# Neighbourhood attention: the second part of the keys in a tile of its own for each head, with zeros in the other 64 rows

## The chip, the cores and the metric

The kernel runs on one core of a Trainium2 chip. The metric is the device time of one execution in microseconds. One execution was also recorded by the hardware profiler; its span is the time from the first to the last instruction.

## The reference

Two layers of a diffusion block over 512 latent tokens (a grid of 8 rows and 64 columns) and 256 context tokens, 1024 features. Each layer mixes the tokens with four groups of heads (gated delta rule, short convolution, long convolution, neighbourhood attention), each 256 features wide, and joins them in one output projection; an MLP follows. The change lies in the neighbourhood attention, with 4 heads of 64 features. Cut to what matters:

```python
qb = qx.reshape(bsz, N_HEADS, rows, ncb, NA_QCOLS, HEAD_DIM) * scale
s_win = jnp.einsum("bhrnqd,bhrwnkd->bhrnqwk", qb, kb)       # 16 query columns against 32 key columns, all 8 rows
s_win = jnp.where(valid[:, :, None, :], s_win + bias, NEG)
s_ctx = jnp.einsum("bhrnqd,bhcd->bhrnqc", qb, kc)           # and against the 256 context tokens
p_all = jax.nn.softmax(jnp.concatenate([s_win..., s_ctx], axis=-1), axis=-1)
o = einsum(p_win, vb) + einsum(p_ctx, vc)
```

In the first layer the context tokens attend to each other as well.

## The kernel before

Large products run on operands split into two parts of a reduced float format, a high part and the small rest, so that high times high, high times rest and rest times high together give nearly the full precision (`mm3`, lines 138 to 140).

`na_project` writes the parts of queries and keys, and the values, to scratch in DRAM. `na_heads` reads them back. It loops over the two pairs of heads (`pr`); for each pair, per head (`sub`), the tile `naq` holds on 64 rows the first part of the queries and on the other 64 rows their second part, and `nak` holds the first part of the keys twice, on both halves. One product over 128 rows (line 1198) thus sums both parts of the queries against the first part of the keys. The second part of the keys, for both heads of the pair, lies in one tile `nakl`; a second product (line 1199) adds the queries' first part times it, on the 64 rows of that head.

A unit is one block of 128 queries of one head. For `n` below 4 the queries are 16 columns of the grid, with two score products of 256 columns each (window, context); in layer 0 the blocks `n` = 4 and 5 are context tokens, with one. That makes 24 units in layer 0, with 40 pairs of lines 1198 and 1199, and 16 units with 32 pairs in layer 1. After the scores of a unit come, in turn: the bias `nab` added on VectorE (line 1207, its load is line 1206), the maximum (1209), the exponential on ScalarE (1212), the reciprocal (1213), the scaling (1217 on ScalarE, or 1215 on VectorE), four transposes on TensorE (1220), the copy of the result to `PT` on ScalarE (1222), and the products with the values (1229), which for the two heads fill 64 columns of the array each. The values come through `vw`, a copy by GpSimd (1174) of a column window of `nav`, transposed on TensorE (1180).

All loads go through SP's queue, in order. Each engine's order is fixed when the program is built, by a planner that weighs dependencies and free buffers; it places the short convolution's products (tiles mc and mx of lines 138 to 140) and others between the units. A tile's tag names a ring of buffers: a new tile of that tag waits until the users of the oldest one are done. `deep` is 0 in layer 0 and 1 in layer 1. GpSimd's zeroing of another tile, line 877, and the modulation rows of line 254 appear in the prediction as well; line 126 and 127 make the two parts of a block of weights.

Of the kernel before, what the change touches and what calls it, by code (L numbers as in the profile page):

```python
# [45 lines left out]
class Net:  # L46
# [24 lines left out]
    def setup(self):  # L71
# [7 lines left out]
        # minus one on one block of 32 or 64 partitions  # L79
# [50 lines left out]
    def split(self, x, y, r):  # L130
        """x as two parts, into the columns r of the pair y."""
        self.nc.scalar.copy(y[0][:, r], x)
        self.nc.vector.tensor_sub(y[1][:, r], x, y[0][:, r].bitcast(F32))

    def mm3(self, o, st, mv, first, last):
        """o (+)= st.T @ mv with both operands as sums of two parts."""
        mmul = self.nc.tensor.matmul
        mmul(o, st[0], mv[0], start=first, stop=False)  # L138
        mmul(o, st[0], mv[1], start=False, stop=False)  # L139
        mmul(o, st[1], mv[0], start=False, stop=last)  # L140

    def pair(self):
        """Two banks of PSUM."""
        return self.pb.tile([128, 2, 512], F32, tag="pb", name="pb", bufs=3)

    def big(self, wsrc, acts, segs):
        """Products of one block of output features; returns a PSUM tile per token range."""
# [19 lines left out]
    def mod_first(self, p, i, act, cb=None):  # L167
        """One block of the shift (i < 2) or scale of the first norm. Few rows: four parts of the sum share the
        array's columns. The weights of some blocks lie where the normed activations will go."""
# [29 lines left out]
    def first_scale(self, XS, p):  # L199
        """Each block of 128 features of the input: features onto partitions, in place, with unit norms."""  # L200
# [39 lines left out]
    def cond_rows(self, p):  # L240
        """The activated conditioning vectors as rows on every partition."""
        self.cbc = p.tile([128, 2, D], F32, tag="cbc", name="cbc")
        self.junk = p.tile([128, 512], BF16, tag="junk", name="junk")
        self.ring(p, "ad", 2)
        self.nc.sync.dma_start(self.cbc, self.cdr[0].partition_broadcast(128))

    def mod_steps(self):
        """One step per block of rows."""
# [19 lines left out]
    def ring(self, p, tag, bufs):  # L268
        """Where the blocks of modulation weights are loaded from now on."""
# [7 lines left out]
    def fac_pre(self, l, i, cnd, k0=0, k1=KB):  # L277
        """gain * (1 + m) of the norm before a sub-layer; i = 0 mixing, 1 mlp."""
# [4 lines left out]
    def fac_post(self, l, i, cnd, p):  # L283
        """gain * m of the norm after a sub-layer, as a row on every partition."""
# [21 lines left out]
    def post_norm(self, Y, row, X, out, p):  # L306
        """out = X + norm(Y) * gain * m for one block of tokens; returns what ends it, which returns a free buffer."""
# [14 lines left out]
    def finish(self, t, mm, ws, Y, row, X, p, before):  # L322
        """The last products and norm of one block of tokens, by halves of the features; before() ends the block
        before. Returns what ends this one."""
# [23 lines left out]
    def pre_scale(self, X, t, p):  # L348
        """The identity times the reciprocal norms."""
# [5 lines left out]
    def pre_norm(self, l, i, xs, p, out, off, cnd, dgs=None):  # L355
        """Features onto partitions; h = norm(x) * gain * (1 + m) + m' as two parts."""
# [59 lines left out]
    def filters(self, ld, p):  # L416
        """The filter networks up to their last hidden layer, two side by side on the partitions: both layers' of the
        long filter, and both halves of the short one's times."""
# [19 lines left out]
    def spectrum_loads(self, l, L, p):  # L438
        """What a filter's spectrum is made from."""
# [10 lines left out]
    def spectrum(self, hs, ld, l, L, p):  # L450
        """Spectrum of a two-sided filter at the odd frequencies and the norm of each channel."""
# [35 lines left out]
    def spectra(self, dft, uc, us, L, p, sp):  # L487
        """The cosine and sine sums over the even and odd times, E +- O, at the odd frequencies:
        [128 k, (C+, C-, S+, S-), k block, channel]. The frequencies of the second block mirror those of the first:
        there the sums over the times 1 and 3 modulo 4 trade cosines for sines, the others only signs."""  # L490
# [5 lines left out]
        if nk == 2:  # L496
            # (source, cosines or sines, parity, where the sum and the difference go)
# [39 lines left out]
    def hyena_project(self, l, w_in, hx, segs, p):  # L537
        """The convolved projections: x1 * v (two blocks) and x0 (two blocks)."""
# [21 lines left out]
    def hyena(self, l, u, x0, segs, ydst, p):  # L560
        nc, a = self.nc, self.a
        for off, L in segs:
# [43 lines left out]
            # the sums of both blocks that belong to each residue of the time: [(residue, cosine or sine)]  # L606
# [25 lines left out]
    def gdn_project(self, l, nm, j0, w_in, hx, segs, psum):  # L632
        """One of q, k and v: projected, convolved, activated and turned to tokens on partitions."""
# [18 lines left out]
    def gdn_rates(self, l, w_ab, hx, segs, p):  # L652
        """The logs of decay and beta, tokens on partitions. Few columns: four groups of them share the array,
        each with its part of the sum."""
# [27 lines left out]
        def rates(after):  # L682
# [6 lines left out]
            # log(1 + e) = log(w) + (e - (w - 1)) / w with w = fl(1 + e)  # L689
# [13 lines left out]
    def gdn_normalise(self, tok, p, rates):  # L703
        """Unit norm and rotary of keys and queries in place."""
# [44 lines left out]
    def gdn_solve(self, l, tok, la, lbeta, p, values):  # L749
# [3 lines left out]
        # feature-major q and k: [2 heads x 64, pair, tokens]  # L753
# [13 lines left out]
        # cumulative log decay, forward and backward, and the total of each block  # L767
# [47 lines left out]
    def gdn_systems(self, kT, qT, nq, p, ip):  # L815
        """Per direction, block and head: the system's strictly triangular part, transposed, and the query
        weights."""
# [35 lines left out]
    def gdn_inverse(self, UX, p, ip):  # L853
        """UX holds N (strictly triangular parts and a diagonal that is ignored); becomes (I + N)^-1."""
        nc = self.nc
        # the diagonal 32-blocks; slots without a system still pass through the 32 x 32 transposes
# [5 lines left out]
        for dr in range(2):  # L862
# [6 lines left out]
            # the blocks with rows before columns for the first direction, after for the second: both lower  # L869
            nc.vector.transpose(S[:, dr] if dr == 0 else S[:, dr].rearrange("p j i -> p i j"),  # L870
                                G[:, dr].rearrange("p u i -> p i u"))
        # the blocks between the halves go apart, zeros in their place and on the diagonal
# [9 lines left out]
        # substitution inside the 32-blocks, both directions at once  # L882
# [7 lines left out]
        # back: G[32 b + j, u, i] = T[i, j] and its transpose GT  # L890
# [11 lines left out]
    def gdn_levels(self, UX, G, GT, Xt, BB, ip):  # L902
        """From the inverses of the 32-blocks to those of 64 and of 128. Every sum runs over all partitions, with
        zeros in all but one block, which keeps the array at its full clock; the directions and blocks work on
        different columns of it at the same time."""
# [4 lines left out]
        def lower(zp, w, signs):  # L910
            """The products of one stage, negated; a part per block of partitions."""
# [11 lines left out]
        # 32 -> 64: block (a, b) of each pair  # L923
# [38 lines left out]
        # 64 -> 128  # L962
# [25 lines left out]
    def gdn_chain(self, dr, X, qk, ring, tok, seen, nq, p):  # L988
        """The blocks of one direction in turn; yields between stages, so that two directions can alternate.
        The sum of both directions takes the place of the queries."""  # L990
# [13 lines left out]
        def decayed(st):  # L1004
            """Keys and queries times their decay from the start of the block, features on partitions."""
# [109 lines left out]
    def na_project(self, w_in, hx, segs, full, dst):  # L1115
        """Queries and keys as two parts, and the values; one step per block of output features."""
# [26 lines left out]
    def na_heads(self, l, src, y, p, pn, with_ctx):  # L1143
# [7 lines left out]
        for pr in range(2):  # L1151
# [3 lines left out]
            # per head: both parts of the queries, and the keys' first part against each; the keys' second part  # L1155
            # lies with the queries' first
            kl = p.tile([128, T], F32R, name="nakl", tag="nakl")
            nc.sync.dma_start(kl.bitcast(F32), src["k", pr, 1])
            qs, ks = [], []
            for sub in range(2):  # L1160
                q = p.tile([128, T], F32R, name="naq", tag=f"naq{sub}")
                k = p.tile([128, T], F32R, name="nak", tag=f"nak{sub}")
                rows = slice(64 * sub, 64 * sub + 64)
                for half in range(2):
# [4 lines left out]
                ks.append(k)  # L1169
            vk = p.tile([128, 10, 128], F32, name="vk", tag="vk")  # L1170
            for n in range(5):
                if n < 4:
                    vw = p.tile([128, 256], F32, name="vw", tag="vw", bufs=2)
# [9 lines left out]
            for n in range(nq):  # L1183
# [3 lines left out]
                for sub in range(2):  # L1187
                    h = 2 * pr + sub
                    rows = slice(64 * sub, 64 * sub + 64)
# [7 lines left out]
                    def score(o, keys):  # L1197
                        nc.tensor.matmul(o, q, keys(ks[sub]), start=True, stop=False)  # L1198
                        nc.tensor.matmul(o, q[rows], keys(kl)[rows], start=False, stop=True)  # L1199
# [4 lines left out]
                    if n < 4:  # L1204
                        bias = p.tile([128, 256], F32, name="nab", tag="nab", bufs=3)
# [18 lines left out]
                # the heads share the array's columns  # L1224
# [59 lines left out]
    def mix(self, l, hx):  # L1284
# [17 lines left out]
        with self.pool("tok") as self.tp:  # L1302
# [12 lines left out]
            with self.pool("gdn") as gp:  # L1315
# [9 lines left out]
                with self.pool("psg", 4, space=PSUM) as self.pg, self.pool("pso", space=PSUM) as self.po:  # L1325
                    na = self.na_project(w_in[14:20], hx, segs, full, nad)

                    def others(n):
                        """Work that fills the gaps of the inverse, and the values."""
# [28 lines left out]
    def mlp(self, l, ysp, ysp_s):  # L1358
# [7 lines left out]
        def runs(ts):  # L1366
            """Neighbouring tiles with the same modulation."""
# [266 lines left out]
def _blocks(w, nb):  # L1634
    """[K, N] -> [N / 128, 128, K / 128, 128]: one contiguous tile per block of outputs."""
# [4 lines left out]
def _layout(x, c, ctx, c_ctx, ada_w, ada_b, norm_pre_mix, norm_post_mix, norm_pre_mlp, norm_post_mlp,  # L1640
# [34 lines left out]
    # relative position bias, gathered for the queries (row, column) of a column block and its key window  # L1675
# [34 lines left out]
```

## Time and profile before

| | us |
|---|---|
| three runs, median | 1896.51 |
| lowest and highest of them | 1891.33 and 1897.97 |
| profiled execution, span | 1898.1 |
| TensorE busy in it | 1804.4 |
| VectorE busy in it | 1269.1 |
| ScalarE busy in it | 775.0 |

No other time of the profiled execution is given beside its span. Busy times of TensorE are modelled at their ends, since matmuls are pipelined: the distance between the starts of two matmuls tells more than the duration of one. A wait is put down to the work that ended it. PE is TensorE's matmuls, PEld its weight loads, DVE VectorE, ACT ScalarE, POOL GpSimd, SP the engine that issues the loads.

### The profile page before, as it was taken

To read this page: it belongs to the slowest core of one execution; us is meant where nothing else is said; L and a number is where in the kernel's file an instruction comes from. 1 tells how busy PE (TensorE), PEld (TensorE's weight loads), DVE (VectorE), ACT (ScalarE), POOL (GpSimd) and SP (SyncE) were. 2 spreads that over 40 slices of the span, in tenths; PEclk is the share of its full clock that TensorE was granted. 3 is DMA by queue.
4 is the path that set the end of the run, shared out by engine and by line. 5 is a ranking of instruction groups with operands and counts; after the bars stand their busy time and mean duration, and the time that the engine had idled before them with its cause. 6 is when DMAs were issued, how large, how long until landed. Compare 5 with 4: busy or idle time off the path is not lost. (4 is left out here: it accounts for less than half of the span.)

```text
span 1898.1 us, 29470 instructions
## 1 busy us (share of the span) xinstructions
PE 1804.4 (95%) x11170; PEld 1450.4 (76%) x11170; DVE 1269.1 (67%) x2366; ACT 775.0 (41%) x1547; POOL 256.7 (14%) x265
## 2 busy tenths in 40 slices
PE   5899888999999999999999999998899999999998
PEld 2577777777779888888888876777676788777876
DVE  3888989665766777755555586779856665454545
ACT  4433553366556222222222263363346563332323
POOL 0202441500022000000000041152230110000002
PEclk9999999999999999999999999989999999999999
DMA  8452312344555434444434233112233664232322
GB/s 276 145 177 83 121 42 98 120 134 129 166 181 180 146 116 127 131 125 128 133 124 132 78 130 131 62 64 84 77 98 112 194 198 127 83 117 72 106 89 83
DMA packets 107073, 233.54 MB, mean 123 GB/s; under 512 B 14929, under 2 KB 19859, under 8 KB 105652
## 3 DMA queue, kind: packets, MB, share of 16 engines
q1 hardware_dynamic: 106932, 231.67, 38.7%
q8 instruction: 88, 1.44, 0.3%
q14 instruction: 53, 0.43, 0.1%
HBM read 208.41 MB, written 23.21 MB: 122 GB/s over the span
## 5 line engine op out<-in xcount | busy, mean ns | idle before, releaser
L126 ACT CAST whi<-raw 128x512 fp32r<-128x512 f32 x444 | 273.6, 620 | 671.6 <-PE pb L140 261.8
L127 DVE TENSOR_TENSOR wlo<-raw,whi 128x512 fp32r<-128x512 f32 x444 | 316.9, 720 | 215.9 <-ACT whi L126 209.7
L140 PE MATMUL pb<-acth,wlo 128*128 128x512 f32 (+2 forms) x808 | 282.6, 350 | 0.0
L139 PE MATMUL pb<-actl,whi 128*128 128x512 f32 (+2 forms) x808 | 282.2, 349 | 0.0
L138 PE MATMUL pb<-acth,whi 128*128 128x512 f32 (+2 forms) x808 | 281.4, 348 | 0.0
L138 PE MATMUL pb<-whi,hid 128*128 128x512 f32 x628 | 249.6, 397 | 0.1
L139 PE MATMUL pb<-wlo,hid 128*128 128x512 f32 x628 | 248.7, 396 | 0.5 <-DVE wlo L127 0.4
L140 PE MATMUL pb<-whi,hid 128*128 128x512 f32 x628 | 248.6, 396 | 0.0
L1497 DVE TENSOR_TENSOR acc<-acc,pb 128x1024 f32<-128x1024 f32 x96 | 117.2, 1221 | 150.5 <-PE pb L140 149.5
L258 DVE SCALAR_TENSOR_TENSOR junk<-adrow,cbc 128x512 bf16<-128x512 f32 x256 | 181.1, 707 | 5.1 <-DMA adrow<-in_adaD_dram 1.8
L139 PE MATMUL mx<-actl,whi 128*128 128x512 f32 x416 | 174.3, 419 | 1.4 <-POOL actl L374 1.1
L138 PE MATMUL mx<-acth,whi 128*128 128x512 f32 x416 | 170.3, 410 | 2.1 <-ACT acth L235 1.2
L140 PE MATMUL mx<-acth,wlo 128*128 128x512 f32 x416 | 171.7, 413 | 0.5 <-DVE wlo L127 0.4
L138 PEld LDWEIGHTS pb<-acth,whi 128*128 128x128 f32 x808 | 152.5, 189 | 20.3
L139 PEld LDWEIGHTS pb<-actl,whi 128*128 128x128 f32 x808 | 152.1, 188 | 20.1
L140 PEld LDWEIGHTS pb<-acth,wlo 128*128 128x128 f32 x808 | 152.5, 189 | 19.7
L374 POOL TENSOR_TENSOR actl<-et,acth 128x256 fp32r<-128x256 f32 (+2 forms) x64 | 56.1, 892 | 745.1 <-DVE et L373 740.4
L138 PEld LDWEIGHTS pb<-whi,hid 128*128 128x128 f32 x628 | 117.7, 187 | 32.4 <-ACT hid L1398 5.1
L140 PEld LDWEIGHTS pb<-whi,hid 128*128 128x128 f32 x628 | 117.8, 188 | 29.5 <-DVE hid L1399 1.8
L139 PEld LDWEIGHTS pb<-wlo,hid 128*128 128x128 f32 x628 | 117.8, 188 | 28.7 <-DVE wlo L127 1.6
L138 PEld LDWEIGHTS mx<-acth,whi 128*128 128x128 f32 x416 | 79.9, 192 | 20.1 <-ACT acth L235 1.6
L139 PEld LDWEIGHTS mx<-actl,whi 128*128 128x128 f32 x416 | 80.5, 194 | 19.1 <-POOL actl L374 1.8
(396 smaller groups left out, 3033.7 us busy)
## 6 DMA issues: line engine op xcount, KB each, us to landing
raw<-in_w_dram SPq DMA_DIRECT2D x276, 256.0 KB, 2.9
adrow<-in_adaD_dram SPq DMA_DIRECT2D x80, 512.0 KB, 3.7
raw<-in_win_dram SPq DMA_DIRECT2D x104, 256.0 KB, 2.8
raw<-in_wout_dram SPq DMA_DIRECT2D x64, 256.0 KB, 3.0
X<-xdr SPq DMA_DIRECT2D x14, 512.0 KB, 4.6
X<-in_xin_dram SPq DMA_DIRECT2D x12, 512.0 KB, 4.4
xdr<-X SPq DMA_DIRECT2D x10, 512.0 KB, 2.9
adp<-in_adaP_dram SPq DMA_DIRECT2D x16, 256.0 KB, 5.4
```

What stands on the lines that cost most here:

```text
L126: self.nc.scalar.copy(hi, raw)
L127: self.nc.vector.tensor_sub(lo, raw, hi.bitcast(F32))
L138: mmul(o, st[0], mv[0], start=first, stop=False)
L139: mmul(o, st[0], mv[1], start=False, stop=False)
L140: mmul(o, st[1], mv[0], start=False, stop=last)
L258: nc.vector.scalar_tensor_tensor(self.junk, raw[:, hs], 1.0, self.cbc[:, cnd, hs], op0=OP.mult, op1=OP.mult, accum_out=self.part[:, l, cnd ...
L374: nc.gpsimd.tensor_sub(lo[:, r], t, hi[:, r].bitcast(F32))
L1497: op = nc.vector.tensor_add(o, o, ps)
```

## The change

The second part of the keys gets a tile for each head (`nakl0`, `nakl1`). Its 64 rows of that head are loaded from DRAM; GpSimd writes zeros to the other 64 rows. Line 1199's product then runs over all 128 rows of `naq`: the rows with the queries' second part meet zeros. The loads of the second part become two of 64 rows instead of one of 128. `vw` no longer has a ring of two buffers of its own, but shares that of the biases `nab`, which has two buffers in layer 0 and three in layer 1, where the biases alone had three in both. The rest of the diff takes comments out.

```diff
@@ -1152,25 +1152,27 @@
             e = T if with_ctx else TX
             vt = p.tile([128, T], F32, name="nav", tag="nav")
             nc.sync.dma_start(vt, src["v", pr])
-            # per head: both parts of the queries, and the keys' first part against each; the keys' second part
-            # lies with the queries' first
-            kl = p.tile([128, T], F32R, name="nakl", tag="nakl")
-            nc.sync.dma_start(kl.bitcast(F32), src["k", pr, 1])
-            qs, ks = [], []
+
+
+            qs, ks, kls = [], [], []
             for sub in range(2):
                 q = p.tile([128, T], F32R, name="naq", tag=f"naq{sub}")
                 k = p.tile([128, T], F32R, name="nak", tag=f"nak{sub}")
+                kl = p.tile([128, T], F32R, name="nakl", tag=f"nakl{sub}")
                 rows = slice(64 * sub, 64 * sub + 64)
+                nc.gpsimd.memset(kl[64 - 64 * sub:128 - 64 * sub].bitcast(F32), 0.0)
+                nc.sync.dma_start(kl[rows].bitcast(F32), src["k", pr, 1][rows])
                 for half in range(2):
                     hr = slice(64 * half, 64 * half + 64)
                     nc.sync.dma_start(q[hr, :e].bitcast(F32), src["q", pr, int(half != sub)][rows, :e])
                     nc.sync.dma_start(k[hr].bitcast(F32), src["k", pr, 0][rows])
                 qs.append(q)
                 ks.append(k)
+                kls.append(kl)
             vk = p.tile([128, 10, 128], F32, name="vk", tag="vk")
             for n in range(5):
                 if n < 4:
-                    vw = p.tile([128, 256], F32, name="vw", tag="vw", bufs=2)
+                    vw = p.tile([128, 256], F32, name="vw", tag="nab", bufs=2 + deep)
                     nc.gpsimd.tensor_copy(vw.rearrange("p (r c) -> p r c", c=32),
                                           vt[:, :TX].rearrange("p (r c) -> p r c", c=64)[:, :, starts[n]:starts[n] + 32])
                 else:
@@ -1186,7 +1188,6 @@
                 PTs = []
                 for sub in range(2):
                     h = 2 * pr + sub
-                    rows = slice(64 * sub, 64 * sub + 64)
                     unit += 1
                     if not with_ctx and unit % 3 == 0:
                         sc = self.pm.tile([128, nk], F32, tag="mc", name="sc", bufs=self.mbufs[1])
@@ -1196,13 +1197,13 @@
 
                     def score(o, keys):
                         nc.tensor.matmul(o, q, keys(ks[sub]), start=True, stop=False)
-                        nc.tensor.matmul(o, q[rows], keys(kl)[rows], start=False, stop=True)
+                        nc.tensor.matmul(o, q, keys(kls[sub]), start=False, stop=True)
                     if n < 4:
                         score(sc[:, 0:256].rearrange("p (r c) -> p r c", c=32),
                               lambda k: k[:, :TX].rearrange("p (r c) -> p r c", c=64)[:, :, starts[n]:starts[n] + 32])
                     score(sc[:, nk - 256:nk], lambda k: k[:, TX:T])
                     if n < 4:
-                        bias = p.tile([128, 256], F32, name="nab", tag="nab", bufs=3)
+                        bias = p.tile([128, 256], F32, name="nab", tag="nab", bufs=2 + deep)
                         nc.sync.dma_start(bias, a["nab"][l, h, variant[n]])
                         nc.vector.tensor_add(sc[:, 0:256], sc[:, 0:256], bias)
                     mx = p.tile([128, 1], F32, name="mx", tag="mx", bufs=4)
```

## Rows read from the trace of the kernel before

**Rows 1.** Page, part 1: busy time, share of the span, instructions.

```profile
PE 1804.4 (95%) x11170; PEld 1450.4 (76%) x11170; DVE 1269.1 (67%) x2366; ACT 775.0 (41%) x1547; POOL 256.7 (14%) x265
```

**Rows 2.** Windows: width, busy PE, PEld, DVE, ACT, POOL (instructions), PEclk, DMA share, GB/s.

```profile
400.00:430.00 30.00, 30.00 (x183) 21.46 (x181) 20.29 (x57) 20.86 (x50) 0.00 (x0) 1.00 0.37 114
430.00:470.00 40.00, 39.99 (x246) 28.64 (x244) 20.00 (x57) 25.41 (x64) 0.81 (x2) 1.00 0.44 122
...
1420.00:1460.00 40.00, 40.00 (x234) 27.41 (x233) 23.50 (x60) 28.56 (x66) 1.06 (x2) 1.00 0.45 128
```

**Rows 3.** Timeline of PE: start, duration, line, operation.

```profile
391.74 0.28 PE L1198 MATMUL sc<-nak,naq 128*128 128x256 f32 x1
391.95 0.38 PE L1199 MATMUL sc<-nakl,naq 64*128 64x256 f32 x1
392.26 0.38 PE L1198 MATMUL sc<-nak,naq 128*128 128x256 f32 x1
...
393.11 0.28 PE L139 MATMUL mc<-actl,whi 128*128 128x256 f32 x1
393.23 0.28 PE L140 MATMUL mc<-acth,wlo 128*128 128x256 f32 x1
...
394.41 0.40 PE L138 MATMUL mx<-acth,whi 128*128 128x512 f32 x1
```

**Rows 4.** Chain that ended last, 1405 to 1475 us, by line.

```profile
by line: PE op L1229 15.3%; PE sc L1199 14.3%; PE mx L139 11.7%; PE pt L1220 11.1%; PE sc L1198 11.1%; PE mx L140 10.5%; PE mx L138 10.5%; DMA raw<-in_wout_dram 5.1%; PE pt L1180 3.8%; issue 1.9%; ACT ysp L132 1.6%; ACT frow L295 1.5%; DVE 
```

**Rows 5.** Instructions of line 1199 and line 1198: ns min/median/max.

```profile
L1199 PEld LDWEIGHTS sc<-nakl,naq x72: 182/183/183, 391.9 to 1459.5; 64*128 64x128 f32 x72
L1198 PEld LDWEIGHTS sc<-nak,naq x72: 186/186/192, 391.5 to 1459.2; 128*128 128x128 f32 x72
```

**Rows 6.** Timeline of PE around line 1229.

```profile
406.67 0.28 PE L140 MATMUL mc<-acth,wlo 128*128 128x256 f32 x1
406.88 0.43 PE L1229 MATMUL op<-PT,vk 128*64 128x128 f32 x2
...
443.62 0.39 PE L1199 MATMUL sc<-nakl,naq 64*128 64x256 f32 x1
443.94 0.43 PE L1229 MATMUL op<-PT,vk 128*64 128x128 f32 x2
```

**Rows 7.** Windows of line 1199 alone: busy PE and PEld (instructions).

```profile
400.00:430.00 30.00, 6.11 (x16) 2.93 (x16) 1.00 0.37 114
...
1420.00:1460.00 40.00, 9.93 (x26) 4.75 (x26) 1.00 0.45 128
```

**Rows 8.** Waits, 391 to 470 us: total, times, longest.

```profile
DVE sc L1207 <- PE sc L1199: 14.5, 13, 3.1
...
PEld op L1229 <- ACT PT L1222: 1.8, 7, 0.4
```

**Rows 9.** Page's DMA part: KB each, us from issue to landing.

```profile
nab<-in_nab_dram SPq DMA_DIRECT2D x32, 128.0 KB, 2.4
nak<-nak SPq DMA_DIRECT2D x16, 192.0 KB, 5.0
...
nakl<-nak SPq DMA_DIRECT2D x4, 384.0 KB, 3.9
```

**Rows 10.** Waits of SP's queue, 384 to 470 us.

```profile
SPq L1206 <- DVE sc L1207: 32.4, 11, 8.0
```

**Rows 11.** Timeline of layer 1's second pair.

```profile
1441.89 0.43 DVE L1207 TENSOR_TENSOR sc<-sc,nab 128x256 f32<-128x256 f32 x1 [0.44 <-PE sc L1199]
...
1442.80 0.44 PE L1180 MATMUL pt<-cst,vw 128*128 128x128 f32 x2
```

**Rows 12.** GpSimd's memset of line 877; timeline of the first vw.

```profile
L877 POOL MEMSET BB<- x4: 1377/1586/1792, 251.5 to 1283.8; 64x1536 f32 x4
...
381.97 0.74 POOL L1174 COPY vw<-nav 128x256 f32<-128x256 f32 x2 [12.11 <-PE ops L1068]
...
385.32 0.60 PE L1180 MATMUL pt<-cst,vw 128*128 128x128 f32 x4
```

## The prediction

> **What bounds the kernel now.** I read the page first: TensorE counts as busy for 95% of the span, more than any other engine [rows 1]. Then I cut out the two stretches in which the scores are made, 391 to 470 us (layer 0) and 1405 to 1470 us (layer 1), because a share over the whole span says nothing about them. In three windows there TensorE has no idle time, at a granted clock of 1.00 (the level of 2.4 GHz), while VectorE and ScalarE are busy 50 to 71% [rows 2]. A busy TensorE is no TensorE at its peak, since the ends of its matmuls are modelled; so I read next the starts in its timeline [rows 3]. There the reader is to see two paces. The short convolution's 128-row products of 256 columns (lines 138 to 140, tile mc) start 0.118 us after one another: eleven intervals from 393.11 to 394.41 are 1.30 us. The scores have the same 256 columns, but around each line 1199, whose operands have 64 rows, the pace is 0.21 us before it and 0.31 us after it. The chain that ended last goes through the same instructions: in 1405 to 1475 us lines 1199 and 1198 hold 14.3% and 11.1% of it, and no other engine has a share as large [rows 4]. So a TensorE interval saved here is on the path that sets the end.
>
> **The second product on 128 rows.** Line 1199 stays one instruction for each product, 72 in all [rows 5], with the same 256 columns. The weight load takes 186 ns on 128 rows against 183 ns on 64, so the taller operand costs nothing that the rows show. What can go is the pause on both sides of the 64-row shape. From 391.74 to 393.11 there are five products in 1.37 us [rows 3]; at the pace of 0.118 us they would take 0.59. Two line 1199 thus cost 0.78 us extra, 0.39 each. 72 times 0.39 is 28.1 us. Behind 7 of the 72 in the timeline comes line 1229, which fills 64 columns of the array, 0.32 us later in the case shown; a part of that pause stays, since behind a 128-row product line 1229 also comes only after 0.21 us [rows 6]. 0.21 instead of 0.12 at one end, and no pause of the next 128-row product to save, are 0.19 us less in each, 1.3 us for 7. Gross gain: 26.8 us, some 15 in layer 0 (40 products) and 12 in layer 1 (32). Its bounds are 0, if the 0.31 us belongs to something that stays, and 28. I take 26.8, because the pause follows every one of the 72 whatever comes next and whichever bank it writes, and none of the 128-row products around them.
>
> A rule speaks against the edit: the Trainium skill, TensorEngine Tiling (Array Packing), section Performance Considerations (When to Use Tiling), would have a contraction of 64 rows use half of the array, so that two such products run beside each other. By it the zeros give away up to half of the work of 72 products, 36 times 0.118 = 4.2 us, and the kernel would end near 1901. The trace does not bear it out for this order: the heads' 64-row products never stand side by side, a 128-row product is always between them, and the pace is the slower one [rows 3]. The Trainium skill's same page, section Key Properties, has a change of the tiling mode drain the engine, which agrees with these rows.
>
> **What lies behind the gain: the softmax.** TensorE's order is fixed when the program is built, so less work between scores and transposes means less cover for the softmax. In 1420 to 1460 us stand 26 line 1199 [rows 7]: 26 times 0.39 is 10.1 us, which leaves 29.9 of 40, and ScalarE is busy 28.6 us in it [rows 2], 96%. In 400 to 430 us 16 of them leave 23.8 us beside 20.9 of ScalarE, 88%; in 430 to 470 us some 20 leave 32.2 beside 25.4, 79%. Nowhere does ScalarE exceed what is left, but at 96% work in a fixed order waits for each other. TensorE already waits for it in small pieces, 1.8 us for the copies of PT in layer 0 [rows 8]. Lower bound of the loss: nothing, for the planner can put convolution products between. Upper bound: the 10.1 us of the tight stretch and half of layer 0's gain, 17 us. I take 4 us, 3 of them in layer 1.
>
> **The shared ring of nab and vw.** Before, the biases had three buffers and vw two of its own; now they share two in layer 0 and three in layer 1. Within a pair of heads a bias load can be issued only when line 1207 of the unit two before has ended; it takes 2.4 us to land [rows 9]. A unit makes two line 1199, so 1420 to 1460 us hold 13 units, 3.1 us each, and 2.3 us each when shortened [rows 7]: two of them, 4.6 us, are nearly twice what the load needs, and in layer 0 the units are no faster. All 13 waits of line 1207 are for the scores, none for a bias [rows 8]. SP's queue already stands 32.4 us at the head of these loads [rows 10], and what is queued behind it are weights for line 126, the next modulation rows and the second pair's keys. At the change of the pair the ring costs more: the second pair's four vw copies must wait for the first pair's last biases, and its first biases for the transposes of vw. In layer 1 the second group of these transposes stands at 1442.8 us, and line 1207 needs its first bias at 1441.9 [rows 11]; a load issued behind it lands over 3 us late, unless the planner moves the transposes up. In layer 0 the context units (n = 4 and 5), which use no bias, stand between. Bounds: nothing, and 4 us in each layer. I take 3 us together.
>
> **Zeros and loads.** Eight memsets of 64x768 on GpSimd: half of line 877's 64x1536, 1.59 us, so 0.79 us each [rows 12]. GpSimd is idle there; two of them stand before the vw copies at 381.97 us and make them 1.6 us later; the copies end at 382.7 and TensorE first reads them at 385.3, so I take nothing. Without that cover it is 1.6 us a pair, 6 us in all. The whole load of nakl (384 KB) becomes two halves. The nearest rows are nak's halves, which land 5.0 us after their issue against 3.9 for the whole nakl [rows 9]: if the first scores of each of the four pairs wait for that, it costs 4 times 1.1, 4.4 us. But the first unit no longer needs the second head's half, and convolution products stand before the first scores, so I take nothing, with 4.4 us as the bound. The Trainium skill, DMA: Bandwidth & Descriptors, section Rules for kernel authors, advises against two transfers to the two halves of the partitions, which it says serialize; by it those 4.4 us would be paid and the sum would be 15.6 us. The rows on landing lean that way, but show nothing that waits for it.
>
> **The sum.** 26.8 less 4 less 3 is 20 us. The profiled execution spans 1898.1 us, so 1878; the page gives no other time for it. The median of the three runs is 1896.5, 1.6 less, so I predict 1876.5. The runs themselves lie within 0.35%; 0.5%, 9.5 us, is about what can be told from no change.
>
> **The rivals.**
> 1. The softmax takes the place of the pauses. For: ScalarE at 96% of the shortened stretch. Against: TensorE waits little for it now. With the upper loss of 17 us, and 3 for the ring, 7 us are left: 1890.
> 2. The whole gain is kept, or a new order gives more: 1866 to 1870. For: TensorE has no real waits there now.
> 3. The change does not remove the pause, because strided keys or accumulation into the same bank makes it: 1896 to 1898. Against: the contiguous keys have it too, and products into other banks after it.
> 4. Slower: the ring of two in layer 0. If each bias load waits behind another load in SP's queue until its scores are done, a unit pays 2.4 us of landing, 16 units 38 us, and 12 us are lost in the end: about 1908. It decides from 1.7 us of lateness a unit (27 over 16). Against: the loads are issued two units ahead.
> 5. Half-row products are the cheap ones: the pauses have another cause and stay, and the zeros add 36 times 0.118, 4.2 us: 1901. Against: the pace around a lone 64-row product is the slower one [rows 3]. (The Trainium skill, TensorEngine Tiling (Array Packing), When to Use Tiling, is the rule behind it.)
>
> **How the numbers follow.** The forecast (1872 to 1884) has 0.55; rival 1 0.18, two thirds of it below 1887; rival 2 0.13; rival 3 0.05; rival 4 0.06; rival 5 0.03. Faster by over 0.5%: 0.55 + 0.13 + 0.12 = 0.80. Within: 0.06 + 0.05 + 0.03 = 0.14. Slower: 0.06. Range: 1866, the whole gain, to 1890, rival 1; rivals 3 to 5 lie outside, and a little of 1 and 2.
>
> **What the profile after would show.** Starts of line 1198 and its successor 0.12 us apart where they are together; the stretches about 11 and 9 us shorter; two MEMSET of 0.8 us for each pair on GpSimd. Wrong would be: 0.2 to 0.3 us between 128-row scores (rival 3); idle time of TensorE before lines 1220 and 1229 on ScalarE, above 6 us a layer (rival 1); line 1207 waiting for a DMA of nab (rival 4).

## The result and the profile after

The changed kernel's median is 1869.1 us (1866.4 to 1872.1, four runs) against 1897.2 us (1891.3 to 1905.7, four runs) before: ratio 0.9861, 95% interval [0.9835, 0.9886]. In a second comparison it took 1876.0 us (1871.8 to 1876.6) against 1897.6 us: 0.9885 [0.9867, 0.9902]. The range of 1866 to 1890 holds both. The second lies beside the forecast of 1876.5 us; the first, 1869.1 us, lies below the forecast's own band (1872 to 1884), in that of rival 2. Over the two comparisons 22 to 28 us went, of some 1897.

In the changed kernel the score products are lines 1199 (first) and 1200 (second), the bias add is 1208, the transposes 1221, the copy of PT 1223, the value products 1230. The profiled execution spans 1865.8 us. Its busy times, as in [rows 1]:

```profile
PE 1772.8 (95%) x11170; PEld 1435.8 (77%) x11170; DVE 1266.4 (68%) x2366; ACT 773.9 (41%) x1547; POOL 264.8 (14%) x273
```

The count of TensorE's instructions is the same, and 31.6 us of its busy time are gone. GpSimd has the eight new memsets. Where TensorE's time went is seen in its timeline of the first scores (start, duration, line, operation), which answers to [rows 3]:

```profile
387.70 0.28 PE L1199 MATMUL sc<-nak,naq 128*128 128x256 f32 x1
387.82 0.28 PE L1200 MATMUL sc<-nakl,naq 128*128 128x256 f32 x1
387.94 0.28 PE L1199 MATMUL sc<-nak,naq 128*128 128x256 f32 x1
388.05 0.28 PE L1200 MATMUL sc<-nakl,naq 128*128 128x256 f32 x1
388.17 0.28 PE L138 MATMUL mc<-acth,whi 128*128 128x256 f32 x1
388.29 0.28 PE L139 MATMUL mc<-actl,whi 128*128 128x256 f32 x1
```

Every start is 0.12 us behind the last; the 0.21 and 0.31 us around the second product are gone. The weight load of the taller operand takes 188 ns where the 64-row one took 183 [rows 5]:

```profile
L1200 PEld LDWEIGHTS sc<-nakl,naq x72: 187/188/194, 387.7 to 1428.6; 128*128 128x128 f32 x72
```

Windows of the two stretches (width, busy PE, PEld, DVE, ACT, POOL, granted clock, DMA share, GB/s), to set beside [rows 2]:

```profile
395.00:425.00 30.00, 29.44 (x217) 23.47 (x216) 21.31 (x63) 23.71 (x58) 2.60 (x4) 1.00 0.54 146
425.00:455.00 30.00, 30.00 (x214) 24.49 (x213) 19.70 (x53) 20.91 (x50) 0.85 (x2) 1.00 0.39 114
...
1405.00:1435.00 30.00, 28.39 (x221) 21.75 (x219) 21.22 (x53) 24.01 (x58) 2.87 (x5) 1.00 0.58 157
```

TensorE now has gaps: 0.56 us in the first window, 1.61 us in the third. ScalarE is at 79% and 80% there, not at the 96% that the prediction had for layer 1's tight stretch. Waits in 386 to 470 us (the first line) and in 1386 to 1440 us (the others), as engine, what waits, for what: total, times, longest, beside [rows 8]:

```profile
PEld op L1230 <- ACT PT L1223: 2.9, 11, 0.4
...
PEld pt L1221 <- ACT P L1218: 1.7, 2, 1.3
...
DVE sc L1208 <- PE sc L1200: 6.7, 3, 4.2
DVE sc L1208 <- DMA nab<-in_nab_dram: 2.9, 2, 1.9
```

The softmax is waited for a little more than before, and a wait for a bias load is there that was not. In the chain that ended last, 1380 to 1440 us, the scores are down from the 25.4% of [rows 4] to 11.6%:

```profile
by line: PE op L1230 16.1%; PE pt L1221 12.4%; PE mx L139 10.8%; PE mx L138 10.8%; PE mx L140 10.8%; PE sc L1199 6.6%; DMA raw<-in_wout_dram 5.4%; PE sc L1200 5.0%; DMA nab<-in_nab_dram 3.4%; PE pt L1182 3.2%; ACT P L1218 2.3%; ACT ysp L132
```

Two loads are on this chain as well, one after the other: a bias that lands late, and output weights. Behind them ScalarE's cast of these weights (line 126) and its scaling of P follow, and TensorE's transposes wait for the scaling (start, duration, what; then the transposes in the timeline, with TensorE's idle time before them in brackets):

```profile
1416.17 2.01 DMA nab<-in_nab_dram
...
1418.36 3.25 DMA raw<-in_wout_dram
...
1421.71 0.62 ACT whi L126
1422.33 0.63 ACT P L1218
```

```profile
1423.01 0.66 PE L1221 MATMUL pt<-cst,P 128*128 128x128 f32 x4 [0.95 <-ACT P L1218]
```

**Two measures for the rest.** *Stage*: in each layer, from the last start of line 1068 (the products before the scores) to the first start of the output projection. It holds the scores and what follows them in the neighbourhood attention, and the granted clock over it is 1.00 in both kernels. *Extra*: over all second products, the starts' distances before, behind and one further, less the undisturbed pace (0.118 us for 256 columns, 0.235 for 512); each distance counts once, and only those behind a product of 256 or 512 columns. Both are worked out from all of TensorE's starts in each trace:

```
kernel          stage, layer 0   layer 1   sum      extra    ratio to before [95%]
before               104.3        67.1     171.4     28.9
changed               91.8        57.9     149.7      3.9    0.9861 [0.9835, 0.9886]
changed, again        91.2        58.4     149.6             0.9885 [0.9867, 0.9902]
half_rows            105.9        68.5     174.5     29.0    1.0018 [1.0004, 1.0032]
two_and_two           98.0        60.8     158.9     15.7    0.9937 [0.9924, 0.9950]
side_by_side          97.9        60.5     158.4     14.9    0.9922 [0.9901, 0.9942]
ring_only            106.0        67.1     173.1             1.0025 [1.0011, 1.0039]
own_l1                91.2        57.6     148.8             0.9864 [0.9850, 0.9879]
vw_in_p               92.6        57.6     150.1             0.9865 [0.9851, 0.9880]
zeros_once            91.8        58.3     150.1             0.9864 [0.9847, 0.9880]
own_once              91.8        57.6     149.4             0.9892 [0.9873, 0.9911]
dve_scale             90.9        57.9     148.7             0.9874 [0.9855, 0.9892]
kl_pool               91.6        56.7     148.2             0.9887 [0.9869, 0.9904]
no_zeros              91.1        62.1     153.1             0.9899 [0.9884, 0.9914]
```

Two numbers in this table hold something else as well. In the changed kernel's extra of 3.9 us stands the wait at 1423.01 us shown above: there two starts are 1.34 us apart, 1.1 over the pace. Without it the extra is 2.8 us, 1.2 in layer 0 and 1.6 in layer 1. And in layer 0 the planner moved four transposes of line 293 into the stage: twelve stand ahead of the output projection in the changed kernel and in half_rows, eight before and in ring_only. The four take 0.9 us.

The stages are 12.5 and 9.2 us shorter, 21.7 together, or 22.6 without the four transposes. The two profiled spans differ by 32.3 us; the other 10.6 us lie outside the stages. Between the two stages TensorE has nearly the same work in both (5,442 and 5,438 products), and it took 916.6 us at a granted clock of 0.98 before and 910.5 us at 0.99 in the changed kernel:

```profile
485.98:1402.58 916.60, 887.61 (x5442) 734.31 (x5439) 627.61 (x1173) 339.43 (x670) 120.53 (x128) 0.98 0.38 121
```

```profile
470.01:1380.52 910.51, 882.69 (x5438) 728.86 (x5436) 628.45 (x1176) 337.74 (x669) 121.86 (x129) 0.99 0.38 122
```

The granted clock over the span (core, span, mean clock) goes with that; before, changed, and changed again:

```profile
core 0: 1898.1 us, clock 0.982
```

```profile
core 0: 1865.8 us, clock 0.987
```

```profile
core 0: 1874.2 us, clock 0.983
```

The third, at nearly the clock of the first, is 23.9 us shorter than it. Among runs at 0.983 the medians are 1899.9 us (nine of before) and 1876.0 us (three of the changed kernel): 23.9 us again. I read the first comparison's 28 us as some 23 to 24 from the change, and the rest as the clock that these executions were granted; of its four runs of the kernel before no clock is known, so this split is argued and not shown.

### The profile page after: what moved, and what is told of

Same layout as the page of the kernel before. It is cut to its first block, busy times and chain, and to the rows that moved or that the text cites. A ratio compares the mean times of both kernels' runs of the same rounds, so it can differ in the third digit from the quotient of the medians.

```text
span 1865.8 us, 29503 instructions
## 1 busy us (share of the span) xinstructions
PE 1772.8 (95%) x11170; PEld 1435.8 (77%) x11170; DVE 1266.4 (68%) x2366; ACT 773.9 (41%) x1547; POOL 264.8 (14%) x273
```

## The experiments

**The row shape alone.** The changed kernel, with zeros, loads and ring, but its second product on the head's 64 rows again.

```diff
+                    rows = slice(64 * sub, 64 * sub + 64)
...
-                        nc.tensor.matmul(o, q, keys(kls[sub]), start=False, stop=True)
+                        nc.tensor.matmul(o, q[rows], keys(kls[sub])[rows], start=False, stop=True)
```

> All of the change stays (a tile for each head, zeros, split loads, shared ring), but the second product reads only the 64 rows of its head again. Theory 1 (a pause at every change between a 64-row and a 128-row product): the whole gain goes, 1894 to 1902 us, and the pace of 0.31 us behind each second product is back. Theory 3 (the shared ring or the new order of the planner made part of the gain): it stays below 1890 us.

1899.96 us, ratio 1.0018 [1.0004, 1.0032]: the whole gain is gone. TensorE's timeline of the first scores:

```profile
390.03 0.28 PE L1200 MATMUL sc<-nak,naq 128*128 128x256 f32 x1
390.24 0.38 PE L1201 MATMUL sc<-nakl,naq 64*128 64x256 f32 x1
390.55 0.38 PE L1200 MATMUL sc<-nak,naq 128*128 128x256 f32 x1
390.87 0.38 PE L1201 MATMUL sc<-nakl,naq 64*128 64x256 f32 x1
391.18 0.39 PE L138 MATMUL mc<-acth,whi 128*128 128x256 f32 x1
```

The 0.31 us are back with the shape and nothing else. The stages are 24.8 us longer than the changed kernel's, the extra 26.2 us longer when the wait at 1423.01 us is left out: of what the pauses cost, all but some 1.4 us arrives in the stage. Against before, the new zeros, loads and ring cost 3.1 us of stage (2.2 without the four transposes) and 3.4 us (0.8 to 6.1) of time. TensorE is idle for 1.1 us in the two stages, where it was 0.8 before: what the three cost lies in another order of its products, more than in waits.

**Fewer changes of shape.** The kernel before, where a unit makes both 128-row products first and then both 64-row ones.

```diff
...
+                    for i, (o, keys) in enumerate(parts):
+                        nc.tensor.matmul(o, q, keys(ks[sub]), start=i == 0, stop=False)
+                    for i, (o, keys) in enumerate(parts):
+                        nc.tensor.matmul(o, q[rows], keys(kl)[rows], start=False, stop=i == len(parts) - 1)
```

> The kernel before, with the order inside a unit turned: both 128-row products first, then both 64-row products, no zeros and no new tiles. Only 32 units have two pairs, and each goes from four changes of shape to two. Theory 1 (the pause belongs to the change of shape): 32 times 0.39 us less, about 12 us, 1882 to 1889 us, with 0.12 us between the two 64-row products. Theory 2 (a 64-row product is slow by itself): 0.31 us between the two 64-row products, 1894 to 1900 us.

1884.48 us, ratio 0.9937 [0.9924, 0.9950], 12 us less. The timeline (x2 are two products that the view merges):

```profile
391.09 0.40 PE L1202 MATMUL sc<-nak,naq 128*128 128x256 f32 x2
391.42 0.50 PE L1204 MATMUL sc<-nakl,naq 64*128 64x256 f32 x2
391.84 0.39 PE L138 MATMUL mc<-acth,whi 128*128 128x256 f32 x1
392.07 0.28 PE L139 MATMUL mc<-actl,whi 128*128 128x256 f32 x1
```

Five products take 0.98 us (391.09 to 392.07), 0.39 over the pace, where the order before had 0.78 for the same five [rows 3]. The price is thus one of each visit to the 64-row shape, not of each product: 41 visits instead of 72, 31 times 0.39 is 12.1 us. (Where the expectation had 0.12 us between the two 64-row products, that was wrong: they start 0.22 us apart. A visit of two has less to pay at its end.)

**Half-row products of both heads beside each other.** The kernel before, with both heads' 128-row products of a block first, and then all 64-row products, the heads in turn.

```diff
...
+                for part in range(2 if n < 4 else 1):
+                    for sub in range(2):
...
+                        firsts.append((o, q, k1, part))
+                        seconds.append((o, q[rows], k2, part))
...
+                for o, q, k, part in firsts:
+                    nc.tensor.matmul(o, q, k, start=part == 0, stop=False)
+                for o, q, k, part in seconds:
+                    nc.tensor.matmul(o, q, k, start=False, stop=part == np_ - 1)
```

> The kernel before with only TensorE's order changed: for each block of queries both heads' 128-row products come first, then all 64-row products in a row, the two heads' (rows 0 to 63 and rows 64 to 127) in turn. 72 visits to the 64-row shape become 20 (16 of four products, 4 of two). Theory 1 (0.39 us for each visit, and nothing gained inside it): 52 times 0.39 = 20 us less, less up to 5 us because both heads' scores now come at once: 1877 to 1882, ratio 0.989 to 0.992; four 64-row products of a visit start 0.12 us or more apart. Theory 2 (products on different halves of the rows run beside each other, so that half-row products are the cheap ones when they stand together): a pair in the time of one, 36 times 0.118 = 4.2 us less again: 1872 to 1877, ratio 0.987 to 0.989. Theory 3 (the pause belongs to each 64-row product whatever its neighbours): 1892 or more.

1883.63 us, ratio 0.9922 [0.9901, 0.9942]. The edit did not come through whole: the planner put the heads apart again, and there are 40 visits, not 20. That is why the time is that of the experiment before, and neither theory's forecast for 20 visits was put to the test. But in three places products of both heads do stand together. One visit of two products of one head, one of three and one of four, each with what follows it:

```profile
391.77 0.50 PE L1211 MATMUL sc<-nakl,naq 64*128 64x256 f32 x2
392.20 0.39 PE L138 MATMUL mc<-acth,whi 128*128 128x256 f32 x1
...
414.46 0.50 PE L1211 MATMUL sc<-nakl,naq 64*128 64x256 f32 x3
414.89 0.50 PE L139 MATMUL mx<-actl,whi 128*128 128x512 f32 x1
...
1435.99 0.51 PE L1211 MATMUL sc<-nakl,naq 64*128 64x256 f32 x4
1436.42 0.50 PE L140 MATMUL mx<-acth,wlo 128*128 128x512 f32 x1
```

Two, three and four products take the same 0.43 us: the starts of the two heads' products lie 0.00 to 0.01 us apart. So products on different halves of the rows do run beside each other, as the Trainium skill has it (TensorEngine Tiling (Array Packing), Key Properties); here a pair takes 0.22 us, hardly less than two 128-row products (0.236). Theory 2's mechanism is seen; whether a kernel with all its pairs together would reach the zeros' time was not measured.

**The ring alone.** The kernel before, with only the ring that nab and vw share.

```diff
-                    vw = p.tile([128, 256], F32, name="vw", tag="vw", bufs=2)
+                    vw = p.tile([128, 256], F32, name="vw", tag="nab", bufs=2 + deep)
...
-                        bias = p.tile([128, 256], F32, name="nab", tag="nab", bufs=3)
+                        bias = p.tile([128, 256], F32, name="nab", tag="nab", bufs=2 + deep)
```

> The kernel before with only the shared ring of nab and vw. Theory 1: no gain, and a loss of 0 to 3 us as the prediction had it: 1896 to 1901 us. Theory 3 (the ring changes the planner's order for the better): 1885 us or less.

1903.06 us, ratio 1.0025 [1.0011, 1.0039]: 4.7 us (2.1 to 7.4) slower, above the 1896 to 1901 us expected. The stages show 1.7 us of it; where the rest lies was not found. GpSimd's copies of vw now wait for the bias adds, and one bias add for its load (who waits for tile nab: us, times):

```profile
  POOL vw L1174: 55.9, 5
  DVE sc L1207: 1.8, 1
```

**The ring's cost in the changed kernel.** Two kernels undo it: one gives vw its own two buffers in layer 1, the other puts vw into the ring of P.

```diff
-                    vw = p.tile([128, 256], F32, name="vw", tag="nab", bufs=2 + deep)
+                    vw = p.tile([128, 256], F32, name="vw", tag="vw" if deep else "nab", bufs=2)
```

> The changed kernel, with vw in two buffers of its own again in layer 1 only (nab keeps three there; layer 0 has no room). Theory A (the ring's cost of about 5 us lies at the change of the pairs, and above all in layer 1, which has no context units between): 2 to 4 us less than the changed kernel, a ratio to the kernel before of 0.985 to 0.987. Theory B (the cost lies in the two buffers for the biases in layer 0): no change, 0.9875 to 0.989.

```diff
-                    vw = p.tile([128, 256], F32, name="vw", tag="nab", bufs=2 + deep)
+                    vw = p.tile([128, 256], F32, name="vw", tag="P", bufs=2 + deep)
```

> The changed kernel, with vw in the ring of the softmax's P instead of that of nab, in both layers; nab keeps two and three buffers for itself. Theory A (the biases behind the copies of vw are late): 2 to 5 us less than the changed kernel, a ratio of 0.984 to 0.987. Theory C (any ring shared with vw costs about the same): 0.987 to 0.990.

0.9864 [0.9850, 0.9879] and 0.9865 [0.9851, 0.9880]. Both lie where theory A expected them, but so does one of the changed kernel's own two ratios (0.9861 and 0.9885), so the ratio can't decide, and the stages must. In the first, the 2.9 us of layer 1's waiting for bias loads are gone; of line 1208's waits in 1386 to 1440 us this one is left:

```profile
DVE sc L1208 <- PE sc L1200: 7.9, 5, 4.2
```

Yet layer 1's stage is 57.6 us where it was 57.9: TensorE is idle for 1.8 us in it, where it was 1.6 in the changed kernel, in other places. So the late biases are real, and one of them is on the chain that ended last; but other waits, as long, take its place when it goes. In the second kernel layer 1 is 57.6 us too, and layer 0 is 92.6.

**Zeros and loads.** First, the zeros are written once a layer, ahead of the loop over the pairs.

```diff
+        zkl = []
+        for sub in range(2):
+            kl = p.tile([128, T], F32R, name="nakl", tag=f"nakl{sub}")
+            nc.gpsimd.memset(kl[64 - 64 * sub:128 - 64 * sub].bitcast(F32), 0.0)
+            zkl.append(kl)
...
-                kl = p.tile([128, T], F32R, name="nakl", tag=f"nakl{sub}")
+                kl = zkl[sub]
...
-                nc.gpsimd.memset(kl[64 - 64 * sub:128 - 64 * sub].bitcast(F32), 0.0)
```

> The changed kernel, with one tile for each head's second key parts for the whole layer: the zeros are written once, four memsets instead of eight, none at the change of the pairs. By the prediction's step the zeros are hidden: no change within 2 us, a ratio of 0.9865 to 0.989. Rival (GpSimd's memset waits for the first pair's last scores and holds the copies of vw behind it): 2 to 4 us less, 0.984 to 0.987.

Second, the second parts are loaded into both halves in place of the zeros, so that the second product also adds both second parts' product, which the others leave out.

```diff
-                nc.gpsimd.memset(kl[64 - 64 * sub:128 - 64 * sub].bitcast(F32), 0.0)
-                nc.sync.dma_start(kl[rows].bitcast(F32), src["k", pr, 1][rows])
...
+                    nc.sync.dma_start(kl[hr].bitcast(F32), src["k", pr, 1][rows])
```

> The changed kernel without the memsets: the second key parts are loaded into both halves of the tile, as the first parts are, so that the second product adds the product of both second parts, which the kernel before leaves out. Two more half loads for each pair of heads in SP's queue. By the prediction's step loads are hidden: no change within 2 us, 0.9865 to 0.989. Rival (the loads are on the path, as the rule on two halves of the partitions has it): 2 to 5 us more, 0.9895 to 0.991.

Third, the loads of the second parts are issued from GpSimd.

```diff
-                nc.sync.dma_start(kl[rows].bitcast(F32), src["k", pr, 1][rows])
+                nc.gpsimd.dma_start(kl[rows].bitcast(F32), src["k", pr, 1][rows])
```

> The changed kernel, but the two loads of the keys' second parts of a pair are issued from GpSimd's queue and no longer from SP's, where each of the ten loads of a pair takes 0.5 to 0.6 us to issue. Theory 1 (the loads behind them in SP's queue are late on the path, and that is where the kernel with more loads lost its time): the stretches become 1 to 2 us shorter in each layer, ratio 0.985 or below. Theory 2 (the loads have slack, and the kernel with more loads lost its time by another order of TensorE's work): both stretches within 1 us of the changed kernel's 91.5 and 58, ratio 0.986 to 0.989.

Zeros once: 0.9864 [0.9847, 0.9880]. That is in the rival's range (0.984 to 0.987), but the changed kernel's 0.9861 is as well; its stages are 150.1 us, no shorter than the changed kernel's 149.7. Loads from GpSimd: 0.9887 [0.9869, 0.9904]; layer 0's stage is as long as the changed kernel's, layer 1's 1.3 us shorter, which theory 1 wanted in both layers and in the time, and theory 2 in neither. It leaves at most that 1.3 us. No zeros: 1880.66 us, 0.9899 [0.9884, 0.9914]. It was to be 2 to 5 us slower if loads are on the path, and is; but layer 1's stage (62.1 us against 57.9) shows another reason. Its window in the kernel without zeros, and in the changed kernel:

```profile
1390.00:1452.00 62.00, 57.10 (x403) 45.70 (x400) 39.54 (x91) 41.47 (x92) 3.84 (x8) 0.97 0.54 145
```

```profile
1380.00:1438.00 58.00, 56.40 (x411) 44.60 (x408) 40.47 (x91) 41.40 (x92) 6.71 (x11) 1.00 0.56 157
```

TensorE is idle for 4.9 us instead of 1.6, and the granted clock is 0.97 instead of 1.00. Its largest wait there is for the softmax:

```profile
PEld sc L1198 <- ACT P L1212: 3.2, 2, 2.7
```

The planner set another order in which exponentials stand ahead of scores, and no load is on the chain that ended last in this window. What more loads would cost in the changed kernel's own order is not shown by this kernel, and stays open.

**ScalarE's share.** The changed kernel, with the second head's scaling on VectorE in layer 0 as well.

```diff
-                    if sub and not with_ctx:
+                    if sub:
```

> The changed kernel, but in layer 0 too the scaling of the second head's probabilities is done on VectorE, as layer 1 has it: 12 instructions of about 0.63 us leave ScalarE. Theory 1 (part of the gain is lost because ScalarE, 88% busy in the shortened stretch of layer 0, holds TensorE up): layer 0's stretch becomes 1 to 3 us shorter than the changed kernel's 91 to 92 us, the time 0.1 to 0.15% below its 0.986 to 0.989 of the kernel before. Theory 2 (ScalarE is not what ends the waits there; VectorE, 71% busy, is as tight): the same length within 1 us, or up to 3 us longer.

1873.79 us, ratio 0.9874 [0.9855, 0.9892]. The window of 395 to 425 us:

```profile
395.00:425.00 30.00, 30.00 (x219) 24.37 (x217) 21.51 (x60) 20.73 (x49) 2.60 (x4) 1.00 0.37 102
```

ScalarE is busy 3 us less there and TensorE's gap of 0.56 us is gone. But the changed kernel's second profile has no such gap either, and layer 0's stage is 90.9 us where the two profiles of the changed kernel have 91.8 and 91.2. That is theory 2's: ScalarE holds TensorE up by at most 1 us in layer 0.

**Two costs taken away together, and the changed kernel once more.** Own buffers in layer 1 and zeros once a layer; and a repetition.

> The changed kernel with two of its costs taken away together: in layer 1 the copies of the value windows have two buffers of their own again, and the zeros are written once per layer (four memsets, no longer eight). Each alone could not be told from the changed kernel. Theory 1 (each hides a loss of 1 to 2 us which only shows when the other is gone too): 2 to 4 us below the changed kernel, ratio 0.985 or below. Theory 2 (neither lies on the path): ratio 0.986 to 0.989, both stretches within 1 us of 91.5 and 58.

> The changed kernel beside the others on the same chip. All theories: 1866 to 1872 us; the granted clock of each run shows whether the episodes of the lower level differ from those of the kernel before (0.982 in one run each so far) by more than from run to run.

The first has 1875.31 us, 0.9892 [0.9873, 0.9911], stages 149.4: nothing hides behind the other. The repetition, the second comparison above, took 1876.0 us where 1866 to 1872 was expected; its runs' granted clocks are 0.982 to 0.985, those of the first comparison 0.983 to 0.988. No version tried beats the changed kernel by more than the measurement can tell.

## Why the prediction was right

- **The second product on 128 rows: 26.8 us gross, 15 and 12 by layer.** The extra fell from 28.9 us to 2.8 (3.9 with the wait in it), by 26.1: 15.0 in layer 0 and 11.1 in layer 1. Mechanism and size hold. Rival 3 (something else makes the pause) fell with half_rows, where only the shape was put back.
- **The softmax: a loss of 4 us.** This term was too large. From half_rows to the changed kernel the extra falls by 26.2 us and the stages by 24.8: 1.4 us is lost. TensorE's idle time says the same: in the two stages it is 1.1 us in half_rows and 2.4 in the changed kernel. The forecast had ScalarE at 96% of a stretch that was to shrink around work that stays in place; in the new order it came to 80%. Rival 1 fell with this and with dve_scale.
- **The ring: a loss of 3 us; zeros and loads: nothing.** The three together cost 2.2 us of stage without the four transposes. The ring alone costs 1.7 of stage, and 4.7 (2.1 to 7.4) of time. That 3 us came near is in part luck: it was to come from copies and biases that are late at the change of the pair, but from before to half_rows TensorE's idle time grows by 0.3 us only. Bias loads do land late in layer 1 as foreseen, one of them on the chain that ended last, but undoing that gains nothing in the changed kernel, so the ring's share there could not be isolated. The memsets take 0.73 us each, where 0.79 was estimated, and leaving out half of them (zeros_once) gains nothing that can be told; these are GpSimd's first two:

```profile
375.10 0.74 POOL L1163 MEMSET nakl<- 64x768 f32 x1 [8.54 <-PE kS L1029]
378.55 0.73 POOL L1163 MEMSET nakl<- 64x768 f32 x1 [2.72 <-PE ops L1068]
```

- **The two halves of nakl.** They land 4.3 us after their issue, against 3.9 for the whole [rows 9], and moving them to another queue changes no time that can be told. The first scores of the two layers start 9.4 and 8.7 us behind the start of their stages, where it was 10.1 and 8.6 before, and nowhere in the changed kernel is a wait put down to a load of nakl. The 4.4 us that the prediction worked out by the Trainium skill's rule on two transfers to the two halves of the partitions (DMA: Bandwidth & Descriptors, Rules for kernel authors) do not show here.

```profile
nakl<-nak SPq DMA_DIRECT2D x8, 192.0 KB, 4.3
```

- **The sum.** Forecast: 26.8 less 4 less 3, 20 us. Worked out from the runs: 26.1 less 1.4 less 2.2, 22.5 us; the stages give 22.6. (That these two agree is no check, since 1.4 and 2.2 come from the same stages; the spans at one clock, 23.9 us, are.) The term that was most in error is the softmax, by 2.6 us. Rival 2 (the whole gain) describes it better than the forecast did, and the first comparison's 1869.1 us lies in its band; but 2.2 us are paid for the ring, zeros and loads, and what lies beyond 24 us goes with the clock.
- **Rivals 4 and 5.** A bias load is waited for 3.5 us in all, not 38. Half-row products of the two heads run beside each other only where they stand side by side; in the order before they never do. That the pause has another cause than the shape, as rival 5 had it, fell with half_rows.

## What to carry to other kernels

A lone product of another row shape is paid for around it, in the starts of its neighbours; its own duration (0.38 us here against 0.28) shows only a part of the 0.39. Compare the distances of starts with those of like products before calling a busy engine fully used. Either keep one shape, with zeros in the unused rows, or gather the odd shapes, so that fewer visits are made. Where a forecast takes a loss because another engine would be full in the shortened stretch, ask first whether its work there can spread over the stage.

## What the runs showed of the hardware that was not expected

- A visit to the 64-row shape costs about 0.39 us, whether it holds one product or two of the same rows; with both halves of the rows in use, four products take the 0.43 us of two.
- TensorE's granted clock over a run differs between executions of one kernel (0.978 to 0.989 in 47 runs of the kernel before), and the time goes with it. In the profiles of before and changed it is 1.00 in both stages, so that the difference lies outside them. Of before, the nine runs at 0.983 have a median of 1899.9 us, the seven at 0.986 one of 1895.3 us. Why an execution is granted more was not found.
